# Down product of three parts of each SwiGLU as seven block products, with weight operands 512 columns wide

## Chip, cores and metric

One core of a Trainium2 chip runs the whole layer in one launch. The metric is the device time of an execution in microseconds (us); lower is better. The kernel before was executed three times.

## What is computed

A hybrid decoder layer on 512 rows (tokens) of 1024 columns: a SwiGLU, a mixer (causal differential attention beside an SSD scan), and a second SwiGLU, each between two RMS norms and with a residual. The change touches the last matrix product of the two SwiGLUs only:

```python
def swiglu(h, w_gate, w_up, w_down):
    return (jax.nn.silu(h @ w_gate) * (h @ w_up)) @ w_down

x = x + 0.5 * rms_norm(swiglu(rms_norm(x, pre_g), w_gate, w_up, w_down), post_g)
```

Here `h` is 512 x 1024, `w_gate` and `w_up` are 1024 x 2816, `w_down` is 2816 x 1024, all float32.

## The kernel before

**Numbers as pairs.** Every large product runs on float32r operands, and each float32 operand is split into a high part (`hi`, a rounded copy) and a low part (`lo = x - hi`). A product of two split operands is three matmuls, hi x hi, hi x lo and lo x hi, summed in PSUM. For weights `split` (L173) does it: a load of 512 KB into a tile `raw` (four buffers), a cast on ACT into `whi` (L175, four buffers) and a subtraction on DVE into `wlo` (L177, four buffers).

**The SwiGLU.** `ffn` (L206) cuts the 2816 hidden columns into 22 tiles of 128, and these into parts of 2, 4, 4, 4 and 8 tiles (L213). For each tile j of a part, `product` (L217) forms gate and up, transposed: 128 hidden columns on the partitions, 512 tokens along the free dimension, 24 matmuls of 512 columns for each of the two (8 tiles of the contraction, three matmuls each, through `mm3`, L194 to L196), in PSUM banks `pa`. Then ACT takes the SiLU (L257), DVE multiplies (L258, into a tile `at`), ACT casts the hidden tile to its high part (L260) and DVE subtracts for its low part (L261).

**The down product of a part** (L269 to L290): the rows of `w_down` for the part's tiles are loaded whole (one `raw` of 128 x 1024 for each tile) and split. For each of four tiles of 128 tokens and each half of 512 columns, a bank collects tiles x 3 matmuls of 512 columns (L283). In the first part ACT copies the bank to the accumulator `acc` (L288); in the next three, DVE adds the bank to `acc` (L290). `acc` is two tiles of 128 x 2 x 1024 in SBUF. With four tiles, a part has 192 matmuls for gate and up and 4 x 4 x 2 x 3 = 96 for down. The last part, of eight tiles, ends in `halves` (L292) and is not touched.

**What sets the order.** The kernel is written as a program over tiles; a scheduler orders each engine's instructions when the program is built, and each engine then runs its own list in that order. Tiles come from pools with a fixed number of buffers: a new tile waits until the last use of the one in its buffer is over. The PSUM has eight banks: three `pa`, two `pb`, two `pt` (used by transposes elsewhere) and one `po`. All weight loads are issued by SP, in one list.

Of the kernel before, what the change touches and what calls it, by code (L numbers as in the profile page):

```python
# [12 lines left out]
F32R = mybir.dt.float32r  # L13
# [4 lines left out]
P = 128  # L18
D = 1024
S = 512  # L20
# [9 lines left out]
class Layer:  # L30
# [175 lines left out]
    def ffn(s, x, h, wg, wu, wd, gain, finish, prepare, fetch=(), late=()):  # L206

        nc = s.nc  # L210
        acc = [s.blk([P, 2, D]) for _ in range(2)]

        parts = [(0, 2), (2, 4), (6, 4), (10, 4), (14, 8)]  # L213
        assert sum(n for _, n in parts) == DFF // P
        banks = {}

        def product(ps, w, cols, by_pass=False, behind=None):  # L217
            ws = [(w[0][:, k, :], w[1][:, k, :]) for k in range(KT)]
            hs = [[a[:, cols] for a in s.hk(h, k)] for k in range(KT)]
            if not by_pass:  # L220
                for k in range(KT):
                    with s.tc.issue_after(behind) if behind is not None and k >= 5 else nullcontext():
                        s.mm3(ps[:, cols], ws[k], hs[k], k == 0, k == KT - 1)
                return

            for i, (a, b) in enumerate(((0, 0), (1, 0), (0, 1))):
                for k in range(KT):
                    nc.tensor.matmul(ps[:, cols], ws[k][a], hs[k][b], start=i + k == 0, stop=i == 2 and k == KT - 1)  # L228

        lead = [(j, w) for j in range(2) for w in (wg, wu)]  # L230
        lw = {}
        after, ins = s.after, None
        for half in range(2):
            for i, (j, w) in enumerate(lead):
                if half == 0:
                    lw[i] = s.load_j(w, j, after if i in late else None)
                    if i == 1:
                        for f in fetch:
                            f()
                    banks[i] = s.pa() if i < 3 else s.po()  # L240
                if half == 0 and i == len(lead) - 1:
                    ins = prepare()
                product(banks[i], lw[i], slice(256 * half, 256 * half + 256), i == 0, ins if half == 0 else None)
        for pi, (j0, n) in enumerate(parts):
            hid = {}
            for j in range(j0, j0 + n):
                if (j - j0) % 2 == 0:
                    hb = s.blk([P, 4, S], F32R)
                if j < 2:
                    pg, pu = banks[2 * j], banks[2 * j + 1]  # L250
                else:
                    g, u = s.load_j(wg, j), s.load_j(wu, j)
                    pg, pu = s.pa(), s.pa()
                    product(pg, g, slice(0, S))
                    product(pu, u, slice(0, S))
                sg, pr = s.m(tag="cv"), s.m(tag="at")
                nc.scalar.activation(sg, pg, AF.Silu)  # L257
                nc.vector.tensor_mul(pr, sg, pu)  # L258
                hh, hl = hb[:, 2 * ((j - j0) % 2), :], hb[:, 2 * ((j - j0) % 2) + 1, :]
                nc.scalar.copy(hh, pr)  # L260
                nc.vector.tensor_sub(hl, pr, hh)  # L261
                hid[j] = (hh, hl)
            if pi == len(parts) - 1:
                gain()
                s.halves(acc, lambda c: s.load_half(wd, j0 * P, n // 2, slice(c * S, (c + 1) * S)),
                         lambda k: hid[j0 + k], n // 2, ((s.pb, s.pb, s.pa, s.po), (s.pa, s.pa, s.pb, s.pb)),
                         gain, finish)
                continue
            wt = {}  # L269
            for j in range(j0, j0 + n):  # L270
                rd = s.raw([P, D])
                nc.sync.dma_start(rd, wd[j * P:(j + 1) * P, :])
                wt[j] = s.split(rd, [P, D])
            for t in range(NT):
                ts = slice(t * P, (t + 1) * P)
                pd = [s.pb(), s.pb()] if t % 2 == 0 else [s.pa(), s.po()]
                for j in range(j0, j0 + n):
                    hh, hl = hid[j]
                    wh, wl = wt[j]
                    f, l = j == j0, j == j0 + n - 1  # L280
                    for a, w, st, sp in ((hh, wh, f, False), (hh, wl, False, False), (hl, wh, False, l)):
                        for c in range(2):
                            nc.tensor.matmul(pd[c], a[:, ts], w[:, c * S:(c + 1) * S], start=st, stop=sp)  # L283
                at = acc[t // 2][:, t % 2, :]
                for c in range(2):
                    a = at[:, c * S:(c + 1) * S]
                    if pi == 0:
                        nc.scalar.copy(a, pd[c])  # L288
                    else:
                        nc.vector.tensor_add(a, a, pd[c])  # L290

    def halves(s, acc, load, op, pairs, banks, gain, finish, step=None):  # L292

# [665 lines left out]
```

## Time and profile before

| | |
|---|---|
| median of 3 runs | 1089.22 us (1089.11 to 1092.16) |
| profiled execution, its own time | 1091.88 us |
| span of the profiled execution | 1090.1 us |
| mean granted TensorE clock | 0.996 of full speed |
| PE (TensorE matmul) busy | 1068.3 us, 98% of the span, 5131 instructions |
| DVE (VectorE) busy | 548.3 us, 50% |
| ACT (ScalarE) busy | 397.7 us, 36% |

Busy time is the share of the span in which an engine has at least one instruction open. A matmul's own duration in the trace overlaps that of the next one, so what a matmul costs is read from the distance of starts, not from the duration. An engine that is not the bottleneck may idle at no cost. PEld is the loading of a matmul's stationary operand, which overlaps the matmul before it.

### The profile page before, as it was taken

Reading aid. Unit: us, or ns where it says so; the run is one execution under the profiler, and the core shown is the slowest. Engines: PE = TensorE matmul, PEld = TensorE weight load, DVE = VectorE, ACT = ScalarE, POOL = GpSimd, SP = SyncE. Lnnn points to the kernel's source line nnn. Section 1 sums busy time; section 2 is a strip of 40 time slices with the busy share of each in tenths; the row PEclk is TensorE's granted clock in tenths of the full one; section 3 lists DMA queues with packets and bytes.
Section 4 is the critical chain, followed back from the end, with each engine's and each line's share of the span. In section 5 each row is a group of like instructions: output and inputs, shape, how many; then the busy total and the mean of one; then the engine's idle time right before and its main releaser. Section 6 shows DMA issues by size and latency. Waiting matters only on the chain. (4 is left out here: it accounts for less than half of the span.)

```text
span 1090.1 us, 13117 instructions
## 1 busy us (share of the span) xinstructions
PE 1068.3 (98%) x5131; PEld 889.8 (82%) x5131; DVE 548.3 (50%) x862; ACT 397.7 (36%) x673; POOL 81.3 (7%) x116
## 2 busy tenths in 40 slices
PE   6999999999999999999999999999999999999997
PEld 6988888888888887888888768888888888888885
DVE  5333434334333754686889977673324343333344
ACT  5431322213222543565664536455213222222231
POOL 3000000000000210000034340020000000000001
PEclk9999999999999999999999999999999999999999
DMA  8242433315323244544342103333314333143211
GB/s 289 78 123 71 127 94 96 100 48 147 101 98 93 102 144 107 152 136 107 97 132 63 58 1 121 92 97 97 116 58 136 97 97 97 54 140 97 97 39 77
DMA packets 136295, 111.05 MB, mean 102 GB/s; under 512 B 5862, under 2 KB 116522, under 8 KB 136234
## 3 DMA queue, kind: packets, MB, share of 16 engines
q1 hardware_dynamic: 135658, 108.12, 32.8%
q0 software_dynamic: 576, 2.10, 0.5%
q8 instruction: 40, 0.66, 0.2%
q14 instruction: 21, 0.17, 0.1%
HBM read 99.72 MB, written 4.19 MB: 95 GB/s over the span
## 5 line engine op out<-in xcount | busy, mean ns | idle before, releaser
L175 ACT CAST whi<-raw 128x1024 fp32r<-128x1024 f32 x176 | 183.4, 1053 | 492.3 <-PE pa L195 209.4
L177 DVE TENSOR_TENSOR wlo<-raw,whi 128x1024 fp32r<-128x1024 f32 x176 | 216.5, 1237 | 228.0 <-ACT whi L175 222.2
L195 PE MATMUL pa<-blk,whi 128*128 128x512 f32 (+1 forms) x864 | 331.0, 383 | 0.0
L196 PE MATMUL pa<-blk,wlo 128*128 128x512 f32 (+1 forms) x864 | 329.5, 383 | 0.0
L194 PE MATMUL pa<-blk,whi 128*128 128x512 f32 (+1 forms) x736 | 279.3, 380 | 0.0
L196 PEld LDWEIGHTS pa<-blk,wlo 128*128 128x128 f32 x864 | 162.4, 188 | 32.6 <-issue 1.2
L195 PEld LDWEIGHTS pa<-blk,whi 128*128 128x128 f32 x864 | 162.6, 188 | 31.2 <-issue 0.7
L194 PEld LDWEIGHTS pa<-blk,whi 128*128 128x128 f32 x736 | 138.3, 188 | 26.1
L258 DVE TENSOR_TENSOR at<-cv,pa 128x512 f32<-128x512 f32 x42 | 28.9, 688 | 130.3 <-PE pa L196 130.3
L195 PE MATMUL pa<-wlo,blk 128*128 128x512 f32 x216 | 85.6, 397 | 0.0
L196 PE MATMUL pa<-whi,blk 128*128 128x512 f32 x216 | 85.0, 397 | 0.0
L140 POOL TENSOR_SCALAR r<-ss 128x1 f32<-128x1 f32 x32 | 12.1, 379 | 802.9 <-DVE ss L332 735.8
L283 PE MATMUL pb<-whi,blk 128*128 128x512 f32 x224 | 65.1, 389 | 0.0
L192 PE MATMUL pa<-blk,whi 128*128 128x512 f32 x128 | 51.3, 401 | 0.0
L283 PEld LDWEIGHTS pb<-whi,blk 128*128 128x128 f32 x224 | 41.9, 188 | 8.6
L290 DVE TENSOR_TENSOR blk<-blk,pb 128x512 f32<-128x512 f32 x24 | 15.4, 684 | 64.3 <-PE pb L283 64.3
L195 PEld LDWEIGHTS pa<-wlo,blk 128*128 128x128 f32 x216 | 40.8, 189 | 8.3 <-issue 0.7
L196 PEld LDWEIGHTS pa<-whi,blk 128*128 128x128 f32 x216 | 40.5, 189 | 8.7 <-issue 0.5
L194 PE MATMUL pa<-whi,blk 128*128 128x512 f32 x120 | 47.5, 395 | 0.0
L283 PE MATMUL pa<-whi,blk 128*128 128x512 f32 x112 | 41.3, 389 | 0.0
L283 PE MATMUL po<-whi,blk 128*128 128x512 f32 x112 | 41.3, 389 | 0.0
L192 PE MATMUL pa<-whi,blk 128*128 128x512 f32 x96 | 39.6, 414 | 0.2 <-ACT blk L621 0.2
(208 smaller groups left out, 1360.1 us busy)
## 6 DMA issues: line engine op xcount, KB each, us to landing
raw<-in_ffn_w_gate_dram SPq DMA_DIRECT2D x44, 512.0 KB
raw<-in_ffn_w_up_dram SPq DMA_DIRECT2D x44, 512.0 KB
raw<-in_ffn_w_down_dram SPq DMA_DIRECT2D x44, 512.0 KB
raw<-in_w_in_dram SPq DMA_DIRECT2D x32, 512.0 KB
blk<-kc SPq DMA_DIRECT2D x96, 64.0 KB
raw<-in_w_out_dram SPq DMA_DIRECT2D x12, 512.0 KB
blk<-in_x_dram SPq DMA_DIRECT2D x4, 512.0 KB
x_d<-blk POOLq DMA_DIRECT2D x4, 512.0 KB, 3.1
```

Of the source, the lines that this page charges most:

```text
L140: nc.gpsimd.tensor_scalar(r, ss, mul / n, eps, op0=ALU.mult, op1=ALU.add)
L175: s.nc.scalar.copy(hi, raw)
L177: s.nc.vector.tensor_sub(lo, raw, hi)
L192: mm(ps, a[0], b[0], start=first, stop=False)
L194: mm(ps, a[0], b[0], start=first, stop=False)
L195: mm(ps, a[0], b[1], start=False, stop=False)
L196: return mm(ps, a[1], b[0], start=False, stop=last).ins
L258: nc.vector.tensor_mul(pr, sg, pu)
L283: nc.tensor.matmul(pd[c], a[:, ts], w[:, c * S:(c + 1) * S], start=st, stop=sp)
L290: nc.vector.tensor_add(a, a, pd[c])
```

## The change

For the parts of four tiles (parts 2, 3 and 4 of each SwiGLU, six in all), the down product is formed from 2 x 2 blocks by Strassen's scheme in Winograd's form: the tokens are cut into two halves of 256, the hidden tiles into even and odd ones, the columns of `w_down` into two halves of 512. Seven block products take the place of eight, each of 2 (token tiles of 128) x 2 (hidden tiles) x 3 = 12 matmuls of 512 columns.

- `sums_of_hidden` forms, for a pair of tiles, four sums and differences of blocks of 128 x 256 on DVE, and their split: one cast on ACT and one subtraction on DVE of 128 x 1024. The even tile's second half needs no split of its own.
- `down7` loads the four blocks of weights (512 KB each), forms four differences of them on DVE (T1 to T4, three in place, T2 in a tile `ka`), splits seven operands instead of four, and adds each product's two banks to `acc` as soon as they are there, 14 additions on DVE instead of eight. Three more products (2, 3 and 22) are accumulated on top of product 11 in the same two `pb` banks after these have been read, and product 4 on top of product 1 in the two `pt` banks.
- In the first part and the last nothing changes.

```diff
-                nc.scalar.copy(hh, pr)
-                nc.vector.tensor_sub(hl, pr, hh)
+                c = slice(0, 256) if n == 4 and (j - j0) % 2 == 0 else slice(0, S)
+                nc.scalar.copy(hh[:, c], pr[:, c])
+                nc.vector.tensor_sub(hl[:, c], pr[:, c], hh[:, c])
                 hid[j] = (hh, hl)
+                if n == 4:
+                    if (j - j0) % 2 == 0:
+                        even = pr
+                    else:
+                        hid[j, "S"] = s.sums_of_hidden(even, pr)
...
+            if n == 4:
+                s.down7(acc, hid, wd, j0)
+                continue
...
-                    if pi == 0:
-                        nc.scalar.copy(a, pd[c])
-                    else:
-                        nc.vector.tensor_add(a, a, pd[c])
+                    nc.scalar.copy(at[:, c * S:(c + 1) * S], pd[c])
...
+    def sums_of_hidden(s, even, odd):
+        v = s.nc.vector
+        f = s.k4([P, 4, 256], tag="kb")
+        a11, a21, a12, a22 = even[:, :256], even[:, 256:], odd[:, :256], odd[:, 256:]
+        v.tensor_add(f[:, 0, :], a21, a22)
+        v.tensor_sub(f[:, 1, :], f[:, 0, :], a11)
+        v.tensor_sub(f[:, 2, :], a11, a21)
+        v.tensor_sub(f[:, 3, :], a12, f[:, 1, :])
+        hi, lo = s.k4([P, 4, 256], F32R, "kc"), s.k4([P, 4, 256], F32R, "bc")
+        s.nc.scalar.copy(hi, f)
+        v.tensor_sub(lo, f, hi)
+        return hi, lo
+
+    def down7(s, acc, hid, wd, j0):
+        nc, v = s.nc, s.nc.vector
+        rows = wd[j0 * P:(j0 + 4) * P, :].rearrange("(q e p) f -> e p q f", e=2, p=P)
+        B = {}
+        for e, c in ((0, 0), (1, 0), (0, 1), (1, 1)):
+            r = s.raw([P, 2, S])
+            nc.sync.dma_start(r, rows[e][:, :, c * S:(c + 1) * S])
+            B[10 * e + c + 11] = r
...
+        def product(a, w, bank, first, into):
+            for u in range(2):
+                if first:
+                    ps[bank, u] = (s.pb if bank == 0 else s.pt)()
+                ts = slice(u * P, (u + 1) * P)
+                for q in range(2):
+                    ah, al = (x[:, ts] for x in A[q][a])
+                    wh, wl = (x[:, q, :] for x in w)
+                    for x, y in ((ah, wh), (ah, wl), (al, wh)):
+                        nc.tensor.matmul(ps[bank, u], x, y, start=first and q == 0 and x is ah and y is wh,
+                                         stop=q == 1 and x is al, skip_group_check=True)
+                d = acc[into[0]][:, u, into[1] * S:(into[1] + 1) * S]
+                v.tensor_add(d, d, ps[bank, u])
+
+        w2 = lambda r: s.split(r, [P, 2, S])
+        w11 = w2(B[11])
+        v.tensor_sub(B[11], B[12], B[11])
+        T1 = B[11]
+        T2 = s.k4([P, 2, S])
+        v.tensor_sub(T2, B[22], T1)
+        w21 = w2(B[21])
+        v.tensor_sub(B[12], B[22], B[12])
+        T3 = B[12]
+        v.tensor_sub(B[21], B[21], T2)
+        T4 = B[21]
+        product(11, w11, 0, True, (0, 0))
+        product(12, w21, 1, True, (0, 0))
+        product(2, w2(T2), 0, False, (0, 1))
+        product(1, w2(T1), 2, True, (1, 1))
+        product(3, w2(T3), 0, False, (1, 1))
+        product(4, w2(B[22]), 2, False, (0, 1))
+        product(22, w2(T4), 0, False, (1, 0))
```

Where the instructions stand in the first of the six parts follows. PE, before: the middle of the down product, with the two banks of the third token tile taken up after DVE has read them (`whi`, `wlo` are weights, `blk` the hidden tiles).

```order
L283 MATMUL pa_866<-whi_772,blk_621 128x512
L283 MATMUL pa_866<-wlo_774,blk_621 128x512
L283 MATMUL pb_838<-whi_760,blk_484 128x512 [waits DVE_49]
L283 MATMUL pb_838<-wlo_762,blk_484 128x512
L283 MATMUL pb_838<-whi_760,blk_484 128x512
L283 MATMUL pb_839<-whi_760,blk_484 128x512 [waits DVE_49]
```

PE, after: the end of products 2 and 1 and the beginning of product 3 (`kc` and `bc` are the high and low parts of the sums of hidden blocks, `whi_829` is T2, `whi_847` T1, `whi_867` T3).

```order
L349 MATMUL pb_797<-whi_829,bc_773 128x512 [waits DVE_49]
L349 MATMUL pb_805<-whi_829,bc_773 128x512
L349 MATMUL pt_851<-whi_847,bc_773 128x512
L349 MATMUL pt_859<-whi_847,bc_773 128x512
L349 MATMUL pb_797<-whi_867,kc_626 128x512 [waits DVE_49]
L349 MATMUL pb_797<-wlo_869,kc_626 128x512
```

The last matmul into `pb_797` of product 2 now stands four places ahead of the first of product 3, which writes on in that bank and waits for the addition that reads it.

DVE, before: the end of the part's hidden tiles and the additions of the down product.

```order
L258 TENSOR_TENSOR at_753<-cv_752,pa_703 128x512 [waits PE_49,Activation_49]
L177 TENSOR_TENSOR wlo_780<-raw_776,whi_778 128x1024 [waits DMAHW0_49,Activation_49]
L261 TENSOR_TENSOR blk_621<-at_753,blk_621 128x512 [waits Activation_49]
L290 TENSOR_TENSOR blk_127<-blk_127,pb_782 128x512 [waits PE_49]
L290 TENSOR_TENSOR blk_127<-blk_127,pb_783 128x512 [waits PE_49]
L290 TENSOR_TENSOR blk_127<-blk_127,pa_810 128x512 [waits PE_49]
```

DVE, after, from the fifth of the 14 rows of the same place (L258, L309, the split of T1 and L310 stand ahead of it; `raw_780` holds T3, `raw_782` block 22).

```order
L352 TENSOR_TENSOR blk_127<-blk_127,pb_797 128x512 [waits PE_49]
L263 TENSOR_TENSOR blk_630<-at_762,blk_630 128x512 [waits Activation_49]
L352 TENSOR_TENSOR blk_127<-blk_127,pb_805 128x512 [waits PE_49]
L312 TENSOR_TENSOR kb_767<-at_762,kb_767 128x256 [waits DVE_49]
L177 TENSOR_TENSOR wlo_869<-raw_780,whi_867 128x1024 [waits Activation_49]
L352 TENSOR_TENSOR blk_127<-blk_127,pt_813 128x512 [waits PE_49]
L352 TENSOR_TENSOR blk_127<-blk_127,pt_821 128x512 [waits DVE_49,PE_49]
L315 TENSOR_TENSOR bc_773<-kb_767,kc_772 128x1024 [waits Activation_49]
L177 TENSOR_TENSOR wlo_887<-raw_782,whi_885 128x1024 [waits Activation_49]
L352 TENSOR_TENSOR blk_127<-blk_127,pb_797 128x512 [waits PE_49]
```

Where two operations of DVE stood between the last hidden tile and the additions, sums, splits and additions now alternate.

SP, after: the loads of the part's four weight blocks and of the next part's first gate and up tiles. (`DMAHW0` to `DMAHW7` are the semaphores that the loads signal in turn; `raw_782` signals `DMAHW6`.)

```order
L325 DMA raw_780<-in_ffn_w_down_dram 128x2x512 [waits DMAHW1_49,DVE_49]
L325 DMA raw_782<-in_ffn_w_down_dram 128x2x512 [waits DMAHW2_49,DVE_49]
L185 DMA raw_922<-in_ffn_w_gate_dram 128x8x128 [waits DVE_49]
L185 DMA raw_928<-in_ffn_w_up_dram 128x8x128 [waits DVE_49]
L185 DMA raw_990<-in_ffn_w_gate_dram 128x8x128 [waits DMAHW6_49,DVE_49]
```

The next part's third load takes the buffer of block 22, so buffers are handed on in the order in which their last uses stand (T1, T3, block 22, T4), and the second load, `raw_928`, takes T3's.

## Rows read from the trace of the kernel before

**Rows 1.** The page: busy time, share of the span, instructions of each engine.

```profile
PE 1068.3 (98%) x5131; PEld 889.8 (82%) x5131; DVE 548.3 (50%) x862; ACT 397.7 (36%) x673; POOL 81.3 (7%) x116
```

**Rows 2.** Waits of PE, whole span: total us, times, longest.

```profile
PE pt L160 <- DVE kb L156: 7.7, 1, 7.7
PE pb L696 <- DVE kc L678: 1.8, 1, 1.8
...
PE pa L192 <- ACT blk L621: 0.2, 1, 0.2
```

**Rows 3.** Parts 2 to 4 of the second SwiGLU: us, PE, PEld, DVE, ACT, POOL, clock, DMA.

```profile
799.46:864.74 65.28, 65.28 (x289) 54.05 (x289) 24.64 (x28) 16.59 (x21) 0.00 (x0) 1.00 0.33 97
864.74:930.02 65.28, 65.28 (x289) 54.05 (x289) 24.65 (x28) 16.59 (x21) 0.00 (x0) 1.00 0.32 97
930.02:995.30 65.28, 65.28 (x289) 54.05 (x289) 24.65 (x28) 16.60 (x21) 0.00 (x0) 1.00 0.33 97
```

**Rows 4.** The chain that ended last, two pieces: start us, us, what.

```profile
757.30 2.72 PE pb L283 x12
812.15 5.44 PE pb L283 x24
```

**Rows 5.** Groups by line and shape, DVE: busy us, mean ns, idle before.

```profile
L177 DVE TENSOR_TENSOR wlo<-raw,whi 128x1024 fp32r<-128x1024 f32 x176 | 216.5, 1237 | 228.0 <-ACT whi L175 222.2
L261 DVE TENSOR_TENSOR blk<-at,blk 128x512 fp32r<-128x512 f32 x44 | 30.1, 685 | 0.0
L290 DVE TENSOR_TENSOR blk<-blk,pb 128x512 f32<-128x512 f32 x24 | 15.4, 684 | 64.3 <-PE pb L283 64.3
L555 DVE CUSTOM_DVE_ANT_0 kb<-pb,dd 128x256 f32<-128x256 f32 x8 | 3.3, 422 | 1.2 <-PE pb L554 1.2
L649 DVE TENSOR_TENSOR cbm<-pt,u 128x128 f32<-128x128 f32 x8 | 2.3, 283 | 0.2
```

**Rows 6.** Timeline of DVE in part 3 of the first SwiGLU: start us, us.

```profile
177.08 1.28 DVE L290 TENSOR_TENSOR blk<-blk,pb 128x512 f32<-128x512 f32 x2 [5.97 <-PE pb L283]
...
182.59 2.36 DVE L177 TENSOR_TENSOR wlo<-raw,whi 128x1024 fp32r<-128x1024 f32 x2
```

**Rows 7.** Timeline of all engines around 61 us, part 2 of the first SwiGLU.

```profile
60.60 0.39 PE L195 MATMUL pa<-blk,whi 128*128 128x512 f32 x1
60.61 0.19 PEld L196 LDWEIGHTS pa<-blk,wlo 128*128 128x128 f32 x1
60.83 0.39 PE L196 MATMUL pa<-blk,wlo 128*128 128x512 f32 x1
...
61.03 1.06 ACT L175 CAST whi<-raw 128x1024 fp32r<-128x1024 f32 x1 [3.34 <-PE pa L195]
...
61.26 0.69 DVE L258 TENSOR_TENSOR at<-cv,pa 128x512 f32<-128x512 f32 x1 [2.31 <-PE pa L196]
...
61.99 0.61 ACT L260 CAST blk<-at 128x512 fp32r<-128x512 f32 x1
62.12 1.23 DVE L177 TENSOR_TENSOR wlo<-raw,whi 128x1024 fp32r<-128x1024 f32 x1 [0.17 <-ACT whi L175]
```

**Rows 8.** Waits of all engines, the one of PEld for L678.

```profile
PEld pb L696 <- DVE kc L678: 2.1, 1, 2.1
```

**Rows 9.** Timeline of SP: the issue of one load of 512 KB.

```profile
145.01 0.38 SPq L185 DMA_DIRECT2D raw<-in_ffn_w_gate_dram  x1
```

**Rows 10.** Windows of 0.1 us after it: the last two columns are DMA share and GB/s.

```profile
146.00:146.10 0.10, 0.10 (x2) 0.06 (x2) 0.00 (x0) 0.00 (x0) 0.00 (x0) 1.00 0.15 46
...
148.30:148.40 0.10, 0.10 (x2) 0.07 (x1) 0.03 (x1) 0.10 (x1) 0.00 (x0) 1.00 0.08 21
148.40:148.50 0.10, 0.10 (x2) 0.10 (x1) 0.10 (x1) 0.10 (x1) 0.00 (x0) 1.00 0.00 0
```

**Rows 11.** Timelines of SP, ACT, DVE and PE at the start of the first SwiGLU.

```profile
1.69 0.43 SPq L768 DMA_DIRECT2D blk<-in_x_dram  x1
9.50 1.45 SPq L133 DMA_DIRECT2D ka<-in_ffn_post_g_dram  x1
...
7.92 1.06 ACT L147 ACTIVATE kb<-blk 128x1024 f32<-128x1024 f32 x1 [2.01 <-DMA blk<-in_x_dram]
...
21.94 1.28 DVE L156 SCALAR_TENSOR_TENSOR kb<-blk,r,ka 128x1024 f32<-128x1024 f32 x1 [0.73 <-POOL r L141]
...
24.22 1.03 PE L160 MATMUL pt<-ident,kb 128*128 128x128 f32 x8
```

More of the change, by code (lines that the diff above doesn't have):

```diff
@@ L285, in ffn @@
                 for c in range(2):
-                    a = at[:, c * S:(c + 1) * S]
-                    if pi == 0:
-                        nc.scalar.copy(a, pd[c])
-                    else:
-                        nc.vector.tensor_add(a, a, pd[c])
+                    nc.scalar.copy(at[:, c * S:(c + 1) * S], pd[c])
[11 more added lines that the diff above has]
+        return hi, lo
@@ new lines, in down7, with blocks @@
+    def down7(s, acc, hid, wd, j0):
[6 more added lines that the diff above has]
+            B[10 * e + c + 11] = r
+        def blocks(q):
+            (eh, el), (oh, ol), (sh, sl) = hid[j0 + 2 * q], hid[j0 + 2 * q + 1], hid[j0 + 2 * q + 1, "S"]
+            A = {11: (eh[:, :256], el[:, :256]), 12: (oh[:, :256], ol[:, :256]), 22: (oh[:, 256:], ol[:, 256:])}
+            for i in range(4):
+                A[i + 1] = sh[:, i, :], sl[:, i, :]
+            return A
+        A = [blocks(q) for q in range(2)]
+        ps = {}
+        def product(a, w, bank, first, into):
[29 more added lines that the diff above has]
+        product(22, w2(T4), 0, False, (1, 0))
```

## Prediction, made before the changed kernel ran

> **What bounds the kernel now.** I read the page's first block first: PE is busy for 98% of the span, DVE for half of it [rows 1]. Busy alone proves little, so the waits of PE come next. PE waited for another engine twelve times in all, in nine pairs of lines; the list runs from 7.7 us down to 0.2 us, and the longest is the wait for the first tile of the program [rows 2]. No line of gate, up or down is in it. The windows of three of the six parts show the same from inside: each lasts 65.28 us, PE is busy for all of it at the full granted clock of 2.4 GHz, while DVE works for 24.6 us and ACT for 16.6 us [rows 3]. The chain of waits gives the price of a matmul there: 12 take 2.72 us, 24 take 5.44 us, so 0.2267 us each [rows 4]. A part's 192 + 96 = 288 matmuls make 288 x 0.2267 = 65.29 us, the whole window. So in these parts a matmul less is 0.2267 us less, as long as PE finds its operands and banks ready, and nothing else there has a price.
>
> **What the change takes away.** Eight block products of 12 matmuls become seven: 96 - 84 = 12 in a part, 72 in six parts. PE's list in the changed program is shorter by just these 72, all still 512 wide. 72 x 0.2267 = 16.3 us. The other engines must pay for it, in a part that then lasts 276 x 0.2267 = 62.6 us.
>
> **What it adds to DVE and ACT.** Prices are a 128x1024 operation 1.23 us, a 128x512 one 0.685 us whether it reads PSUM or not, and for 128x256, which has no such row as a plain addition, 0.42 us: the one row of that width shows it [rows 5], and the line through 128x128 (0.283) and 128x512 (0.685) gives the same. Per part on DVE: three more splits and four differences of weights, 7 x 1.23 = 8.6; eight sums of hidden blocks and two splits of them, 8 x 0.42 + 2 x 1.23 = 5.8; six more additions to `acc`, 4.1; less two half splits, 0.5. Together 18.0, so DVE goes from 24.6 to some 43 us of 62.6. ACT gets three casts of weights and two of sums at 1.06 us [rows 7], some 5 us: 22 of 62.6. On the average both stay covered by PE. The loads are the same 2 MB a part.
>
> **Where the average deceives.** The additions and sums crowd behind the part's last hidden tile. I walk through it from zero, the start of the first down matmul. An engine that waits for PE starts 0.43 us after the start of the last matmul it needs (60.83 to 61.26, 60.60 to 61.03 [rows 7]), so DVE begins with the last hidden tile at 0.2. Up to product 3 it then has 13 operations: four of 1024, six of 512, three of 256, 4 x 1.23 + 6 x 0.685 + 3 x 0.42 = 10.3 us. Rows that follow each other start 0.60 us apart where they last 0.684, and 1.13 where they last 1.23 [rows 6], so 12 x 0.09 come off: done at 9.4. PE has 44 matmuls, 10.0 us, until it needs the twelfth of the 13. The tightest point is the cast of the second pair's sums. The eighth operation ends at 0.2 + 5.2 - 0.6 = 4.8, the cast at 5.9, and PE comes to it after 30 matmuls at 6.8, or 6.6 with the loading of the stationary operand (0.19 us [rows 7]). So 0.7 us is left: no wait, but no wide margin.
>
> **The wait that I do expect** is at product 3. It writes on in the bank of product 2, whose last matmul stands four places ahead of it in PE's list. The addition starts 0.43 us after the start of that matmul and lasts 0.68; what waits for DVE follows 0.04 us later (61.26 + 0.69 to 61.99 [rows 7]) and the matmul loads its operand, 0.19: 1.34 us against 4 x 0.2267 = 0.91. That is 0.43 us a part, 2.6 us in six. If the operand is loaded ahead it is 0.25; I take 0.43, since PEld stood waiting together with PE in the one long wait of this kind, 2.1 us beside 1.8 [rows 2, 8]. The other four places at which a bank is taken up again (11 to 2, 12 to 1, 1 to 4, 3 to 22) have 8 to 34 matmuls between, 1.8 us at least, and DVE is there in time by the walk.
>
> The row says that an addition of 0.68 us is hidden when other banks are written meanwhile. The Trainium skill's "Perfetto Trace Analysis", section "Optimizing Tensor Performance", asks that groups of matmuls rotate through different PSUM banks so that the reading of one overlaps the next; this change lets four products write on in banks that have just been read. By the page the cost is the reading itself wherever a bank is reused at once; which is the last rival below; by the walk it is 2.6 us in all.
>
> **The next part's weights.** Split buffers are reused four splits later, so gate and up of the next part wait for products 1 and 3, which end well ahead. Their loads wait for `raw` buffers. SP's list hands the second load T3's buffer, which is free at about 6 us of the walk. A load's traffic ends 3.4 us after its issue (145.01 to 148.40 [rows 9, 10]); with many loads ahead of it the second tile of x took 6.2 us (1.69 to 7.92 [rows 11]). The cast that needs it can't start before product 3 ends, 14 us: covered either way.
>
> **The start.** The loads of two gains (9.50 us [rows 11]) move from the beginning of SP's list behind part 4, so two tiles of x come earlier, and their transposes stand nine matmuls earlier in PE's list. PE went from one to the next there without a wait; the tiles had been ready 1 us ahead (21.94 + 1.28 against 24.22 [rows 11]), and both ends move. I cost it at nothing; at worst it is the 1 us.
>
> **The sum.** 16.3 - 2.6 = 13.7 us. The profiled execution took 1091.88 us with a span of 1090.1; it would take 1078.2. The median of the runs is 2.66 us lower, so 1089.22 - 13.7 = **1075.5 us**, 1.3% less. About 0.3% (3.3 us) is what a measurement of this kernel can tell from no change.
>
> **Rivals.**
>
> *The burst is late.* The walk has 0.7 us of margin at its tightest, over eight dependent steps on two engines. If each loses 0.2 us more than the rows of undisturbed stretches show, PE waits 0.9 us there and as long again at products 1 or 3, some 1.0 to 1.2 a part beyond the 0.43: 13.7 - 6 x 1.1 = 7.1, about 1082. For it: DVE is full for 9 us in a row, which it never is in these parts before. Against: PE's rhythm and DVE's rows are exact there, the three windows agree to 0.01 us [rows 3].
>
> *The up tile is late.* If its load took T4's buffer, the last to be free, it would start only after four additions from 10.4 on (4 x 0.60) and a split, at 14.1; with 3.4 for the load, 1.06 for the cast and 0.2 for the operand PE gets it at 18.8 and stands there after 74 matmuls at 16.8. 2.0 instead of 0.43 a part: 16.3 - 12.0 = 4.3, 1084.9. SP's list speaks against it.
>
> *Each bank stands while it is read* (slower). If DVE comes to the additions only after PE has done the matmuls in between, each of the five places costs the bare handover, 1.34 - 0.23 = 1.11 us: 5.55 a part against 2.72 saved, 6 x 2.83 = 17 us more, 1106. It decides from an additional delay of some 2 us on DVE: the least distance is 1.8 us. That is the page's rule at its full price. Against it: a bank in the kernel before is taken up again too, and PE has no such wait [rows 2].
>
> That the change doesn't do what it says is excluded by PE's list.
>
> **How the numbers follow.** Forecast 0.70, late burst 0.18, late up tile 0.05, bare handovers 0.07. The likeliest gives 1075.5. The range begins a little below no wait at all (1089.22 - 16.3 = 1072.9) at 1072.5 and ends with the late burst at 1082, which leaves out 0.12 above and the worse half of the burst case. Faster by over 0.3% (under 1086): the forecast, nearly all of the late burst and half of the late up tile, 0.90. Within 0.3%: 0.04. Slower: the handovers, less one part in seven for a milder form, 0.06.
>
> **What would show it.** PE 72 instructions fewer; windows of a part at 63.0 us, with DVE at 40 to 43; among PE's waits one on DVE's addition (L352) six times, 0.25 to 0.45 each, and hardly another in these parts. A wait of `pt` or `kc` matmuls on the sums or casts speaks for the late burst; one of `pa` on a cast of weights for the late up tile; waits on L352 at several places in a part for the handovers. The forecast is wrong if a part's window stays above 64 us, or if a matmul of the new products takes other than 0.227 us.

## The result

| | before | changed |
|---|---|---|
| median, measured together (4 runs each) | 1089.38 us (1089.11 to 1092.16) | **1077.27 us** (1075.16 to 1078.38) |
| ratio, with its 95% interval | | 0.9881 [0.9859, 0.9903] |
| profiled execution, its own time | 1091.88 us | 1078.38 us |
| its span | 1090.1 us | 1076.7 us |

The kernel became 1.2% faster. The forecast was 1075.5 us, between 1072.5 and 1082.0; the median lies 1.8 us above it. A second measurement of the same kernel on another occasion (below, with the experiments) gave 1075.11 us and a ratio of 0.9859 [0.9843, 0.9876]; the kernel before had a median of 1091.60 us there. Executions of either kernel differ among themselves by some 3 us; what makes the changed kernel's differ is shown at the end.

The page of the changed kernel, busy time, share and instructions of each engine, beside [rows 1]:

```profile
PE 1054.5 (98%) x5059; PEld 876.2 (81%) x5059; DVE 644.6 (60%) x1000; ACT 427.3 (40%) x703; POOL 82.2 (8%) x116
```

PE has 5131 - 5059 = 72 instructions fewer. DVE works 96 us more, ACT 30 us more, and PE's share stays at 98%: the added work fills idle time of engines that had it.

The windows of parts 2 to 4 of the second SwiGLU, each from its first down matmul to the next part's (the third as far into the last part), with the columns of [rows 3]:

```profile
792.88:855.84 62.96, 62.86 (x277) 51.73 (x276) 40.76 (x51) 21.61 (x25) 0.00 (x0) 1.00 0.34 101
855.84:918.80 62.96, 62.86 (x277) 51.73 (x276) 40.77 (x51) 21.62 (x25) 0.00 (x0) 1.00 0.36 109
918.80:981.76 62.96, 62.86 (x278) 51.74 (x276) 33.70 (x41) 21.00 (x24) 0.00 (x0) 1.00 0.43 125
```

A part takes 62.96 us where it took 65.28. In the first SwiGLU the parts are as long: their first down matmuls start at 92.96, 155.91 and 218.87 us. Six parts save 6 x 2.32 = 13.9 us. That is all that the change gives. The span fell by 13.4: the start happened to be 0.7 us earlier (93.70 to 92.96), and 1.3 us were lost again between the two SwiGLUs, at a clock that fell for longer than in the execution before (see the end).

276 matmuls at 0.2267 us make 62.57 us, so 0.39 us a part is lost. PE's waits, where I meant to find them (total us, times, longest, as in [rows 2]), say nothing of it:

```profile
PE pt L160 <- DVE kb L156: 7.5, 1, 7.5
PE pb L777 <- DVE kc L759: 1.8, 1, 1.8
PE pb L160 <- DVE kb L156: 1.4, 1, 1.4
```

But the same list for PEld, the loading of operands, has them:

```profile
PEld pt L160 <- DVE kb L156: 7.5, 1, 7.5
PEld pb L349 <- DVE blk L352: 3.1, 6, 0.5
```

Six waits of 0.52 us on DVE's addition, one in each part. Their place in the first part, in the timeline of all engines (start us, us, engine, line, what, and the idle time before with what ended it):

```profile
102.93 0.62 PE L349 MATMUL pb<-whi,bc 128*128 128x512 f32 x2
...
103.36 1.28 DVE L352 TENSOR_TENSOR blk<-blk,pb 128x512 f32<-128x512 f32 x2 [0.75 <-PE pb L349]
103.39 0.61 PE L349 MATMUL pt<-whi,bc 128*128 128x512 f32 x2
...
104.10 0.19 PEld L349 LDWEIGHTS pb<-whi,kc 128*128 128x128 f32 x1 [0.52 <-DVE blk L352]
104.10 0.50 PE L349 MATMUL pb<-whi,kc 128*128 128x512 f32 x1
104.21 0.19 PEld L349 LDWEIGHTS pb<-wlo,kc 128*128 128x128 f32 x1
104.44 0.40 PE L349 MATMUL pb<-wlo,kc 128*128 128x512 f32 x1
```

At 102.93 begins product 2's last matmul into the first of its banks, at 104.10 product 3's first into the same bank. Four matmuls would take 0.91 us; it took 1.17, and the next one comes 0.34 us later instead of 0.23: 0.26 + 0.11 = 0.37 us. PE's list misses it because each matmul is drawn 0.39 us long: the one of 103.62 covers the wait up to 104.01, and the 0.09 us that remain do not appear in the list.

DVE's burst behind the last hidden tile of the same part, and the cast of ACT on which the tightest point of the walk rests (the first down matmul starts at 92.96):

```profile
93.23 0.69 DVE L258 TENSOR_TENSOR at<-cv,pa 128x512 f32<-128x512 f32 x1 [3.38 <-PE pa L196]
93.95 0.43 DVE L309 TENSOR_TENSOR kb<-at,at 128x256 f32<-128x256 f32 x1
...
97.57 0.42 DVE L312 TENSOR_TENSOR kb<-at,kb 128x256 f32<-128x256 f32 x1
97.90 1.22 DVE L177 TENSOR_TENSOR wlo<-raw,whi 128x1024 fp32r<-128x1024 f32 x1
99.05 1.28 DVE L352 TENSOR_TENSOR blk<-blk,pt 128x512 f32<-128x512 f32 x2
100.25 1.22 DVE L315 TENSOR_TENSOR bc<-kb,kc 128x1024 fp32r<-128x1024 f32 x1
101.39 1.22 DVE L177 TENSOR_TENSOR wlo<-raw,whi 128x1024 fp32r<-128x1024 f32 x1
```

```profile
98.02 1.05 ACT L314 CAST kc<-kb 128x1024 fp32r<-128x1024 f32 x1 [1.03 <-DVE kb L312]
```

DVE is full from 93.23 to 102.61. The eighth operation ends at +5.0, the cast at +6.1, the thirteenth operation at +9.65; the walk said 4.8, 5.9 and 9.4.

Prices by group on DVE, beside [rows 5]: the 256-wide sums, which the trace before did not have as plain additions, cost what the line through its neighbours gave (0.42 us).

```profile
L352 DVE TENSOR_TENSOR blk<-blk,pb 128x512 f32<-128x512 f32 x48 | 31.8, 682 | 21.1 <-PE pb L349 21.1
L352 DVE TENSOR_TENSOR blk<-blk,pt 128x512 f32<-128x512 f32 x36 | 23.0, 680 | 0.0
L309 DVE TENSOR_TENSOR kb<-at,at 128x256 f32<-128x256 f32 x12 | 5.1, 426 | 0.4
```

### The profile page after: what moved, and what is told of

The parts are those of the page before. It is cut to its first block, busy times and chain, and to the rows that moved or that the text cites. A ratio compares the mean times of both kernels' runs of the same rounds, so it can differ in the third digit from the quotient of the medians.

```text
span 1076.7 us, 13167 instructions
## 1 busy us (share of the span) xinstructions
PE 1054.5 (98%) x5059; PEld 876.2 (81%) x5059; DVE 644.6 (60%) x1000; ACT 427.3 (40%) x703; POOL 82.2 (8%) x116
## 5 line engine op out<-in xcount | busy, mean ns | idle before, releaser
L175 ACT CAST whi<-raw 128x1024 fp32r<-128x1024 f32 x188 | 196.8, 1052 | 405.2 <-PE pa L195 163.7
L177 DVE TENSOR_TENSOR wlo<-raw,whi 128x1024 fp32r<-128x1024 f32 x188 | 231.1, 1234 | 171.0 <-ACT whi L175 168.8
L258 DVE TENSOR_TENSOR at<-cv,pa 128x512 f32<-128x512 f32 x42 | 28.8, 686 | 110.8 <-PE pa L196 110.7
L196 PE MATMUL pa<-whi,blk 128*128 128x512 f32 x216 | 85.5, 400 | 0.0
L194 PE MATMUL pa<-whi,blk 128*128 128x512 f32 x120 | 47.4, 395 | 0.0
L352 DVE TENSOR_TENSOR blk<-blk,pb 128x512 f32<-128x512 f32 x48 | 31.8, 682 | 21.1 <-PE pb L349 21.1
L192 PE MATMUL pa<-whi,blk 128*128 128x512 f32 x96 | 40.1, 419 | 0.2 <-ACT blk L702 0.2
L349 PE MATMUL pb<-whi,blk 128*128 128x512 f32 x96 | 31.5, 389 | 0.0
L194 PE MATMUL pb<-whi,blk 128*128 128x512 f32 x80 | 31.3, 391 | 0.0
L195 PE MATMUL pb<-wlo,blk 128*128 128x512 f32 x80 | 31.1, 389 | 0.0
L196 PE MATMUL pb<-whi,blk 128*128 128x512 f32 x80 | 31.1, 389 | 0.0
```

The source lines that it names most:

```text
L175: s.nc.scalar.copy(hi, raw)
L177: s.nc.vector.tensor_sub(lo, raw, hi)
L192: mm(ps, a[0], b[0], start=first, stop=False)
L194: mm(ps, a[0], b[0], start=first, stop=False)
L195: mm(ps, a[0], b[1], start=False, stop=False)
L196: return mm(ps, a[1], b[0], start=False, stop=last).ins
```

## The experiments

The theory: a part lasts as long as PE's matmuls (0.2267 us each), plus the handing over of one bank at product 3; DVE's and ACT's added work costs nothing as long as the burst behind the last hidden tile stays ahead of PE. All kernels below are the changed one with one edit. The windows of a part are the sharper measure: the six of one kernel agree to 0.1 us (to 0.01 in most), its executions only to some 3 us.

**1. More matmuls between product 2 and product 3**

```diff
+                        with s.tc.issue_after(behind) if behind is not None and u == 1 else nullcontext():
+                            ins = nc.tensor.matmul(ps[bank, u], x, y, ...
...
-        product(2, w2(T2), 0, False, (0, 1))
-        product(1, w2(T1), 2, True, (1, 1))
+        p2 = product(2, w2(T2), 0, False, (0, 1))
+        product(1, w2(T1), 2, True, (1, 1), p2)
```

> The second half (u = 1) of product 1 is held behind the last matmul of product 2, so that eight matmuls instead of three stand between the last one into product 2's bank and product 3's first. Theory (the 0.37 us that PE loses at product 3 in each part is the handing over of that bank: addition and operand take 1.34 us from the start of the last matmul, and 9 x 0.2267 = 2.04 us now lie between): the loss goes, each of the six parts takes 62.58 us instead of 62.95, 276 x 0.2267, and the whole takes 2.2 us less than the changed kernel, about 1075. Rival (the loss comes from the operands, T3's split or the sums, being late): product 3 starts no later than before in PE's list, the loss stays at 0.37 or moves to product 2, whose low part of the sums is now needed 1.1 us earlier; parts at 62.95 or more.

Measured: 1074.25 us (1073.64 to 1074.76), ratio 0.9848 [0.9831, 0.9865]. A part:

```profile
92.64:155.20 62.56, 62.56 (x277) 51.82 (x276) 40.78 (x51) 21.74 (x25) 0.00 (x0) 1.00 0.34 101
```

62.56 us, 276 x 0.2267, and PE full. Around product 3 of the first part, DVE and PE:

```profile
101.07 1.22 DVE L177 TENSOR_TENSOR wlo<-raw,whi 128x1024 fp32r<-128x1024 f32 x1
102.21 1.28 DVE L353 TENSOR_TENSOR blk<-blk,pb 128x512 f32<-128x512 f32 x2
```

```profile
101.48 0.62 PE L350 MATMUL pb<-whi,bc 128*128 128x512 f32 x2
...
103.30 0.39 PE L350 MATMUL pt<-whi,bc 128*128 128x512 f32 x1
103.52 0.39 PE L350 MATMUL pb<-whi,kc 128*128 128x512 f32 x1
```

The addition even starts late here (0.73 us after the matmul, since DVE is splitting), but product 3 comes 2.04 us after the matmul and goes through. Counted from the first down matmul, product 3 begins at 10.88 us (103.52 - 92.64), where the changed kernel began it at 11.14 (104.10 - 92.96). The theory holds, the rival falls: T3 and the sums were never late.

**2. Twelve matmuls put back**

```diff
         product(11, w11, 0, True, (0, 0))
+        spare = s.po()
+        for u in range(2):
+            for q in range(2):
...
+                    nc.tensor.matmul(spare, x, y, start=u + q + i == 0, stop=u + q == 2 and i == 2)
```

> Twelve matmuls of 512 columns are put back into each seven-product part (product 11's operands once more, into the idle bank po, whose content nobody reads); all additions, sums, differences and splits of the change stay. Theory (PE's number of matmuls sets the length of a part, what DVE and ACT do more is free): parts of 288 x 0.2267 = 65.28 us again, the wait at product 3 gone since 13 matmuls now lie there; total that of the kernel before within 2 us (about 1089). Rival (the 18 us more of DVE and 5 us of ACT cost something beyond the 0.37): parts above 65.3, by as much as they cost. Other rival (matmuls that lie beside a wait are free): parts below 65.2.

Measured: 1089.27 us (1089.03 to 1091.87), ratio 0.999 [0.9979, 1.0].

```profile
93.84:159.12 65.28, 65.28 (x290) 54.05 (x289) 41.29 (x51) 21.63 (x25) 0.00 (x0) 1.00 0.32 97
```

The part of the kernel before to 0.01 us, with DVE at 41.3 us instead of 24.6 [rows 3]. So the added work is free here, and the gain comes from the twelve matmuls and nothing else. The new order of PE's list also takes the wait at product 3 away: thirteen matmuls stand between product 2's last one into the bank and product 3's first (104.26 and 107.44 us in this trace). The clean comparison is therefore with experiment 1, which has no such wait either: 65.28 - 62.56 = 2.72 us, twelve times 0.2267. These twelve give the burst more time as well, since they stand ahead of the products that need the sums; what the burst can bear is the next experiment's question.

**3. More work inside the burst: one sum formed twice, and four times**

```diff
-        v.tensor_add(f[:, 0, :], a21, a22)
+        for _ in range(4):
+            v.tensor_add(f[:, 0, :], a21, a22)
```

> The first of the four sums of hidden blocks (128x256) is formed four times instead of once: three more DVE operations for a pair of tiles, 0.35 to 0.42 us each, six in a part, some 2.3 us; DVE then works for 43 of 63 us. The scheduler orders the rest of DVE's list anew: by the order of its list a split of weights (1.13 us) comes to stand ahead of the second pair's sums too, so that these end some 9.5 us after the start of the first down matmul and their cast some 10.6, where PE comes to it after 36 matmuls, 8.2 us. Theory (what counts is the burst behind the last hidden tile, not the average): PE waits 2.4 to 2.9 us a part for the cast; parts of 65.2 to 66.0 us, longer than those of the kernel before. Rival (the average counts: DVE is free for a third of the part): parts of 62.6 to 63.0 us.

> The first of the four sums of hidden blocks is formed twice instead of once: one more DVE operation of 128x256 for a pair of tiles (0.35 to 0.42 us), two in a part. The scheduler puts two splits of weights (1.13 us each) elsewhere in DVE's list by it; by the walk along that list the sums end 6.6 us after the first down matmul and their cast 7.7, just ahead of PE (8.2 less 0.2 for the operand), while the low part of the sums is ready at about 10.2, where PE comes to it at 10.0. Theory (the burst behind the last hidden tile has a few tenths of a us left): parts between 62.95 and 63.6 us. Rival (the average of DVE counts): 62.6 to 62.95. Rival (the margin was already gone in the changed kernel): 63.3 or more, by the whole of the added operations.

Measured: 1092.52 us with four (three more), 1079.78 us with two (one more), a single execution each. Their parts:

```profile
92.67:158.26 65.59, 63.50 (x277) 51.57 (x276) 42.89 (x57) 21.50 (x25) 0.00 (x0) 1.00 0.33 96
```

```profile
92.55:156.02 63.47, 63.18 (x277) 51.64 (x276) 41.43 (x53) 21.53 (x25) 0.00 (x0) 1.00 0.33 100
```

With three more, DVE has 2.1 us more to do, the part takes 2.6 us more, and the whole gain of the change is gone, while DVE idles for 22.7 us of the 65.6. The average says nothing; what stands ahead of the sums in DVE's list does. DVE, ACT and PE there:

```profile
100.61 1.22 DVE L177 TENSOR_TENSOR wlo<-raw,whi 128x1024 fp32r<-128x1024 f32 x1
101.75 0.42 DVE L313 TENSOR_TENSOR kb<-at,kb 128x256 f32<-128x256 f32 x1
102.20 1.04 ACT L315 CAST kc<-kb 128x1024 fp32r<-128x1024 f32 x1 [2.12 <-DVE kb L313]
103.29 0.50 PE L350 MATMUL pb<-whi,kc 128*128 128x512 f32 x1 [1.81 <-ACT kc L315]
103.63 0.40 PE L350 MATMUL pb<-wlo,kc 128*128 128x512 f32 x1
...
106.43 0.50 PE L350 MATMUL pb<-whi,kc 128*128 128x512 f32 x1
```

1.96 + 0.11 us against the rhythm are the wait for the cast of the sums, where I had expected 2.4 to 2.9; 0.45 more arise at a bank of product 12 that product 1 takes up, and the 0.37 at product 3 (106.43) stays: 2.9 of the 65.59 - 62.57 = 3.0 us.

The added sums are not the only thing that makes the cast late. The second pair's sums end 9.50 us after the first down matmul (102.17 - 92.67), in the changed kernel 5.03. Of these 4.5 us the three added sums make 1.0; two splits (2.3) and two additions of banks (1.2) that the scheduler's new order puts ahead of the last sum make the rest. What the added sums alone would cost, in the order of the changed kernel, no run shows; by its trace, as an estimate, the cast would end at 6.1 + 1.0 = 7.1 us, and PE, which comes to it at 6.6, would wait 0.5.

With one more, the size came within what I expected, but by coincidence, for it arose at another place: not the low part of the sums was late, but that same bank of product 12. This kernel, then the changed one:

```profile
98.22 0.62 PE L350 MATMUL pt<-whi,blk 128*128 128x512 f32 x2
...
98.62 0.42 DVE L313 TENSOR_TENSOR kb<-at,kb 128x256 f32<-128x256 f32 x1
...
98.96 1.28 DVE L353 TENSOR_TENSOR blk<-blk,pt 128x512 f32<-128x512 f32 x2
...
99.12 0.39 PE L350 MATMUL pb<-whi,bc 128*128 128x512 f32 x1
...
99.70 0.50 PE L350 MATMUL pt<-whi,kc 128*128 128x512 f32 x1 [0.19 <-DVE blk L353]
```

```profile
98.62 0.62 PE L349 MATMUL pt<-whi,blk 128*128 128x512 f32 x2
...
100.67 0.39 PE L349 MATMUL pt<-whi,kc 128*128 128x512 f32 x1
```

The last matmuls of product 12 into its two banks begin at 98.22 and 98.45, the first of product 1 at 99.70. Two things meet here. DVE is still at a sum, so the addition starts at 98.96 instead of 98.22 + 0.43 = 98.65. And in the scheduler's new order PE comes back to the bank after four matmuls, in the changed kernel after eight (98.62 and 100.67): it would be there at 99.35 and stands 0.35 us, with 0.11 behind it. 63.47 - 62.96 = 0.51 us a part, for 0.7 us more work on DVE; neither run of this experiment changes DVE's work alone, since PE's and DVE's orders change with it.

**4. A bank taken up again after one matmul**

```diff
-        product(1, w2(T1), 2, True, (1, 1))
-        product(3, w2(T3), 0, False, (1, 1))
+        p3 = product(3, w2(T3), 0, False, (1, 1))
+        product(1, w2(T1), 2, True, (1, 1), p3)
```

(`product` holds its matmuls behind the one it is given, as in experiment 1, but for both halves.)

> Product 1 is held behind product 3, so that only one matmul (0.23 us) stands between product 2's last one into its first bank and product 3's first one into the same bank. Theory (the handing over costs 1.34 us from the start of the last matmul into the bank to the next one into it): 1.34 - 2 x 0.2267 = 0.9 us at product 3, instead of 0.37; product 2 comes 1.1 us earlier in PE's list, so that it meets the low part of the sums too early by up to 1.0 us; parts of 63.5 to 64.5 us. Rival (the bank may be written on while it is read, the loss of 0.37 comes from operands): no more than the 1.0 us at product 2, and product 3 follows it without a gap.

Measured: 1087.31 us, one execution; parts of 64.84 us, longer than the 63.5 to 64.5 expected. PE and DVE at the place:

```profile
102.25 0.73 PE L350 MATMUL pb<-whi,bc 128*128 128x512 f32 x2 [0.70 <-DVE bc L315]
103.99 0.50 PE L350 MATMUL pb<-whi,kc 128*128 128x512 f32 x1 [1.00 <-DVE blk L353]
```

```profile
102.11 1.22 DVE L177 TENSOR_TENSOR wlo<-raw,whi 128x1024 fp32r<-128x1024 f32 x1
103.25 1.28 DVE L353 TENSOR_TENSOR blk<-blk,pb 128x512 f32<-128x512 f32 x2
```

The low part of the sums is 0.86 us late, as expected. At product 3 PE loses 1.29 + 0.11 us, more than the 0.9 of the theory: the addition should have started at 102.25 + 0.43 = 102.68, but DVE was splitting until 103.25, 0.57 us longer. From the addition's start to the matmul it is 103.99 - 103.25 = 0.74 us; in the changed kernel 104.10 - 103.36 = 0.74, with one more sum 99.70 - 98.96 = 0.74. So the handing over is 0.43 + 0.74 = 1.17 us, plus 0.11 at the matmul after it, plus whatever DVE has in hand. The rival falls: product 3 does not follow without a gap, it stands until the addition has read the bank. The program's semaphore asks for that (the `[waits DVE_49]` in PE's list); what the chip would do without it, no run shows.

**5. One more part of four, the last one shorter**

```diff
-        parts = [(0, 2), (2, 4), (6, 4), (10, 4), (14, 8)]
+        parts = [(0, 2), (2, 4), (6, 4), (10, 4), (14, 4), (18, 4)]
...
```

(A second hunk keeps the last part, now of four tiles too, in the old form with eight products.)

> The last part of eight tiles is cut in two: one more part of four with seven products in each SwiGLU, then a last part of four in the old form (two more seven-product parts in all, eight instead of six). Theory (a seven-product part costs 62.95 us where eight products would cost 65.28, whatever part it is): 24 matmuls fewer, eight parts with the wait at product 3, 2 x 2.33 = 4.7 us less than the changed kernel, about 1072.6. Rival (the end of a SwiGLU turns into the bound: with four tiles the last four banks come from PE 2.7 us apart instead of 5.4, while DVE's finishing of a token tile, with norms and residual, takes some 3.7 us of operations): 1 to 4 us of waits at each end, so between 1072 and 1080, and the new wait is to be seen after the last down matmuls.

> The two edits together: product 1's second half behind product 2 in each of eight seven-product parts, and the last part cut in two. Theory: a part takes 62.57 us as with the first edit alone, eight parts save 8 x 2.72 = 21.8 us of matmuls with no wait at product 3, about 2 x 2.72 = 5.4 us less than the first edit alone, some 1069. Rival (the ends of the SwiGLUs become the bound, as for the cut alone): what the cut alone loses there is lost here too, and the time lies as far from the first edit alone as the cut alone does from the changed kernel, less 0.7 us.

Measured: 1077.79 us (1077.68 to 1079.13), ratio 0.9884 [0.987, 0.9899], for the cut alone; 1073.91 us (1073.43 to 1074.66), ratio 0.9844 [0.9828, 0.9861], with the edit of experiment 1. The eight parts have their 62.96 and 62.56 us, so the products save what they should; the ends take it back, as the rival said, and neither forecast (1072.6 and 1069) came true. In the second SwiGLU with both edits, DVE:

```profile
1062.64 2.73 DVE L420 SCALAR_TENSOR_TENSOR blk<-blk,r,blk 128x512 f32<-128x512 f32 x4
1065.30 0.68 DVE L405 TENSOR_TENSOR blk<-blk,pb 128x512 f32<-128x512 f32 x1
```

PE's last matmul starts at 1062.72, but the addition of its bank waits until 1065.30 for DVE, which finishes two other token tiles. With experiment 1 alone it starts 0.43 us after the last matmul (1064.52, 1064.95). 2.15 of the 2.72 us are gone. In the first SwiGLU a new wait of 3.0 us for the next norm's rows stands among PE's waits (the second of the two times here, 10.6 - 7.6):

```profile
PE pt L160 <- DVE kb L156: 10.6, 2, 7.6
```

Together 5.15 us, of the 2 x 2.72 = 5.44 that two more parts save. So the cut is worth nothing measurable: 1073.91 against 1074.25 us.

**6. The changed kernel and experiment 1 side by side**

> The changed kernel once more, unaltered, beside the next run and on the same chip. Theory: 12 to 13.5 us less than the kernel before; in its profile again parts of 62.95 us with 0.37 us lost at product 3, while the start of the program (first down matmul at 92.6 to 93.8 us over the runs so far) and the stretch around 640 us may lie up to 1 us elsewhere, since they belong to an execution, not to the change.

> Product 1's second half behind product 2, as in the first experiment, now on one chip with the changed kernel. Theory: six parts of 62.56 us, 6 x 0.39 = 2.3 us less than the changed kernel; rival (what the first experiment gained in the median came from an execution's start and clock, not from the bank): no difference between the two medians beyond 1 us although the parts are shorter.

Measured: the changed kernel 1075.11 us (1074.95 to 1077.69), ratio 0.9859 [0.9843, 0.9876]; with product 1's second half behind product 2, 1074.36 us (1073.81 to 1074.70), ratio 0.9847 [0.9833, 0.9861]. The changed kernel lies 16.5 us below the 1091.60 of the kernel before, more than the 12 to 13.5 expected: its parts save 13.9 again, and the rest, as far as the runs show, belongs to the executions: the kernel before by itself had a median of 1089.38 on the first occasion and 1091.60 here. The parts are 62.96 and 62.56 us again. The medians differ by 0.75 us, and the intervals overlap: by them alone the two can't be told apart, as the rival said. The profiled executions, both at a mean clock of 0.998, span 1073.5 and 1072.1 us, while the first down matmul came at 92.78 in the one and at 93.75 in the other: 1.4 + 0.97 = 2.37 us, the 6 x 0.39. So the better order is worth 2.4 us in the parts, and the later start hid about 1 us of it in these executions.

## Why the prediction was right

- **What bounds the kernel; 72 x 0.2267 = 16.3 us.** Right: with the twelve matmuls of a part put back (experiment 2) it takes 65.28 us, without them and without a wait (experiment 1) 62.56.
- **The wait at product 3, 0.43 us a part.** Right in place, cause and number (six); 0.37 in size. The mis-sized piece is the end of its chain: from the addition's start to the matmul I added 0.68, 0.04 and 0.19 to 0.91 us, and three kernels show 0.74, with 0.11 for the matmul behind it. The operand's loading does not stand between them as a step of 0.19: PEld's row and PE's begin together at 104.10, and the matmul is drawn 0.11 longer. So the wait itself is 0.26 us, the 0.25 that the prediction gave for an operand loaded ahead and did not take. Experiment 1 removes the wait and nothing else.
- **DVE to some 43 us, ACT to 22.** 40.8 and 21.6. DVE's is less because I added up durations, while rows that follow each other overlap by 0.09 us.
- **The tightest point, 0.7 us at the cast of the sums.** 6.6 - 6.1 = 0.5 us in the trace; no wait. Experiment 3 shows how little can upset it: three more sums, with the order that the scheduler then chose, cost 2.6 us a part, most of it at this cast; one more costs 0.5, but at a bank.
- **The next part's weights and the start, both at nothing.** No wait on weights in the parts. The start came 0.7 us earlier, but one kernel in two executions gives 92.64 and 93.75, so no effect of the change can be told from that.
- **The sum.** 13.7 us forecast, 13.9 in the parts. That the first median lies 1.8 us above 1075.5 comes, as far as the runs show, from the executions and not from a term: the second one is 1075.11. That this one lies so near to 1075.5 is in part luck, since it depends on whether the clock fell in an execution (see the end); what the prediction got right is the 13.9 us of the parts.
- **The rivals.** The late burst did not come, but experiment 3 brings it about with 2.1 us of work more a part and the order of the lists that went with it, to 1092.5 us; it is the case that was near. The late up tile did not appear. Bare handovers at five places did not either: one place of five had to wait, for 0.37 us. (Against this rival the prediction used PE's list of waits [rows 2], which, as it turned out, does not show waits this short; the window that is full to 65.28 us [rows 3] does bear it out.) The advice in the Trainium skill's "Perfetto Trace Analysis" (section "Optimizing Tensor Performance") to rotate banks is borne out in direction by experiments 1 and 4. The traces add the size here: a bank came up again 1.17 us after the start of its last matmul, plus what DVE had in hand. With nothing in hand, five matmuls of 0.2267 us between would cover that, an estimate from these two numbers.
- **What would show it.** One item failed: the wait on L352 is not in PE's list but in PEld's, at 0.52 us instead of 0.25 to 0.45.

## What to carry to other kernels

Where one engine is full, its instructions times their distance of starts give the gain of leaving some out, and work added to the others was free here on two conditions: in the stretch where they are busy without a break, each result was still ready before PE came to it (0.5 us ahead at the tightest), and no operation that hands a buffer back was held up for longer than PE stayed away. So walk through the densest stretch operation by operation, with the order of each list; the average (a third of DVE idle) would have missed a loss of the whole gain. When a bank or buffer is to be taken up again, count what stands between its last writer and the next one, and move independent work there: eight matmuls between instead of three took the last loss of the parts away.

## What the runs showed of the hardware

A wait shorter than the drawn length of a matmul (0.39 us against a rhythm of 0.2267) leaves next to no idle time of PE (0.09 of the 0.26 us at product 3); it is to be read from the distance of starts or from PEld's waits.

After the longest wait in the middle of the program (1.83 us at L777, and again the same in other kernels) the granted clock fell to half, 1.2 GHz, in some executions and not in others of the same kernel. The changed kernel's two profiled executions, windows after that wait with the clock third from the end:

```profile
630.00:634.00 4.00, 4.00 (x7) 2.49 (x8) 3.15 (x6) 1.21 (x3) 0.51 (x2) 0.50 0.00 0
634.00:638.00 4.00, 4.00 (x15) 3.12 (x14) 0.00 (x0) 0.72 (x1) 0.23 (x1) 0.73 0.00 0
```

```profile
630.00:634.00 4.00, 4.00 (x17) 2.94 (x17) 2.89 (x6) 1.93 (x4) 0.74 (x2) 1.00 0.00 0
634.00:638.00 4.00, 4.00 (x29) 3.62 (x28) 0.75 (x1) 1.46 (x4) 1.66 (x1) 1.00 0.00 0
```

The first, of 1076.7 us, ran at half clock from 629 to 636; the second, of 1073.5, not at all, and between its third part's first down matmul and the second SwiGLU's first it is 3.0 us shorter (570.98 against 574.01). The execution before fell to 0.5 from 638 to 641 (575.04 us on that way, with a part that is 2.3 us longer). So of the 3.2 us between these two executions 3.0 lie in the stretch with this wait, and the clock behind it is the difference that the windows show. The other executions fit: the changed kernel's spans on the second occasion are 1073.2 to 1073.5 us at a mean clock of 0.998 and 1076.0 at 0.996; the kernel before's there are 1087.3 at 0.998 and 1089.4 to 1090.7 at 0.995 or 0.996. What decides whether the clock falls after the same wait stays open.
